# Storing the low parts of the weights from ACT's queue instead of SP's, in a two-layer hybrid trunk

## The chip, the cores and the metric

The kernel runs on one core of a Trainium2 chip. The metric is the device time of one execution in microseconds. The engines are named as in the profile: PE (TensorE, matmul; PEld is its weight load), DVE (VectorE), ACT (ScalarE), POOL (GpSimd) and SP (SyncE, which here only issues DMAs). An engine works through its own list of instructions in order; a DMA is issued from such a list too, so an issue that waits for something holds up what stands behind it on that engine.

## The reference

Two layers over x of 1024 tokens by 1024 channels, all in float32:

```python
h = rms_norm(x, g_pre)
z = h @ w_in            # 3532 columns, split among four mixers
mix = concat(nsa_attention(...)   * silu(gate_a),
             spatial_gating(...)  * silu(gate_b),
             conv_module(...)     * silu(gate_c),    # 31 taps, causal
             rwkv7(...)           * silu(gate_d))    # recurrence over tokens
x = x + rms_norm(mix @ w_out, g_post)
x = x + gated per-layer embedding (two products with weights)
```

The attention has compressed, selected and window branches. RWKV-7 is a recurrence over tokens; in chunks of 64 tokens it needs the inverse of a triangular matrix.

## The kernel before

**Tiling.** Channels lie on partitions. The tokens of each layer l are done in two halves (h=0 and h=1) of 512. Weights come in granules of 128 x 512 elements (256 KB), and every big product is done with three matmuls (`mm3`, L166 to L170): each operand is split into a rounded high part and a low part, and high x high, high x low and low x high are added in PSUM. Such a matmul has the form 128x128 by 128x512.

**A granule** goes through `split_w` (L147 to L164). SP loads it to `ws` (L152), ACT makes the rounded copy `wh` (L158), POOL subtracts to give the low part `wl` (L160). There are three buffers of each. In h=0 the low part is also stored to DRAM (L163, tiles `low0` to `low143`), so that in h=1 SP loads it (L157) instead of POOL making it again. That is 144 stores, 140 of 256 KB and 4 of 152 KB.

**The triangular solve** of RWKV (`rwkv_solve`, L457 to L498) is done once in each half. The matrices go to DRAM (`Nd`) and come back in another layout: four loads of `LB` (L471) and four of `L2` (L476) on SP. DVE does two substitutions: the first over `LB` (L484, L486), the second over `L2` in 16 steps, each a product (L506) and a sum (L508). ACT transposes the results (L492, L510) and issues sixteen small DMAs (`put`, L496) into `Xd`. In `rwkv_tri` SP loads a chunk of the inverse from `Xd` (L536), and the recurrence on PE begins with it (L540, then L547). Its chain has copies on ACT at L527, L595, L602 and L629.

**Other names.** L694 is a tap of the convolution on DVE; L678 and L679 make its input. L976 is ACT's copy of the transposed softmax, which PE multiplies with the values at L981; L1035 is the exponential. L1076 stores intermediate tiles `ped` from ACT's queue.

**Order.** The lists of all engines are set when the kernel is built, by a scheduler which goes by dependencies and priorities; the body of `split_w` has its priority raised by 4000. A DMA also waits for the eighth DMA before it in the list of both queues, since eight semaphores are used in turn.

Of the kernel before, what the change touches and what calls it, by code (L numbers as in the profile page):

```python
# [8 lines left out]
F32 = mybir.dt.float32  # L9
# [32 lines left out]
class Trunk:  # L42
    def __init__(self, ctx, tc, a):
        self.ctx, self.tc, self.nc, self.a = ctx, tc, tc.nc, a
        nc = self.nc
        self.dram = ctx.enter_context(tc.tile_pool(name="dram", bufs=1, space=bass.MemoryType.DRAM))
        self.cp = ctx.enter_context(tc.tile_pool(name="consts", bufs=1))
        self.sb = ctx.enter_context(tc.tile_pool(name="sb", bufs=1))
        self.pp = ctx.enter_context(tc.tile_pool(name="pp", bufs=1, space=bass.MemoryType.PSUM))
        self.n = 0  # L50
        self.nd, self.wide, self.xq, self.xs = 0, None, None, None
        self.low, self.keep = {}, True
        self.setup()

    BUFS = {"aT": 16, "ws": 3, "wh": 3, "wl": 3, "t2": 7, "y": 7, "rv": 2, "pt": 3, "r4": 4, "ab": 8,
# [91 lines left out]
    def split_w(self, src, cols, key, keep):  # L147
        nc = self.nc
        with self.tc.high_priority(offset=4000):
            st = self.t([128, 512], "ws")  # L150
            for ap, w in src:
                nc.sync.dma_start(ap(st), w)  # L152
            hi = self.t([128, 512], "wh", dt=F32R)
            lo = self.t([128, 512], "wl", dt=F32R)
            kept = self.low.get(key)
            if kept is not None:
                nc.sync.dma_start(lo[:, :cols].bitcast(F32), kept)  # L157
            nc.scalar.copy(hi[:, :cols], st[:, :cols])  # L158
            if kept is None:
                nc.gpsimd.tensor_sub(lo[:, :cols], st[:, :cols], hi[:, :cols].bitcast(F32))  # L160
            if kept is None and keep:
                kept = self.low[key] = self.dram.tile([128, cols], F32, name=f"low{len(self.low)}")
                nc.sync.dma_start(kept, lo[:, :cols].bitcast(F32))  # L163
        return hi, lo  # L164

    def mm3(self, out, lh, ll, rh, rl, first, last, shared=False):  # L166
# [1165 lines left out]
```

## Time and profile before

| what | us |
|---|---|
| median of 3 runs | 1803.48 (1800.02 to 1820.78) |
| the profiled execution | 1808.38 |
| its span in the trace | 1806.7 |
| PE busy | 1680.6 (93%) |
| DVE busy | 1210.3 (67%) |
| ACT busy | 796.9 (44%) |
| POOL busy | 398.4 (22%) |
| SP's queue waiting at the stores L163 | 365.5 |

Issues of DMAs don't count as busy. A wait is put down to the instruction whose end came last before the waiting one began. Idle time of an engine that PE does not wait for costs nothing. The mean granted clock of TensorE in this execution was 0.965 of full speed (2.4 GHz); 0.5 is its lower level.

### The profile page before, as it was taken

To read this page: it belongs to the slowest core of one execution; us is meant where nothing else is said; L and a number is where in the kernel's file an instruction comes from. 1 tells how busy PE (TensorE), PEld (TensorE's weight loads), DVE (VectorE), ACT (ScalarE), POOL (GpSimd) and SP (SyncE) were. 2 spreads that over 40 slices of the span, in tenths; PEclk is the share of its full clock that TensorE was granted. 3 is DMA by queue.
4 is the path that set the end of the run, shared out by engine and by line. 5 is a ranking of instruction groups with operands and counts; after the bars stand their busy time and mean duration, and the time that the engine had idled before them with its cause. 6 is when DMAs were issued, how large, how long until landed. Compare 5 with 4: busy or idle time off the path is not lost. (4 is left out here: it accounts for less than half of the span.)

```text
span 1806.7 us, 29182 instructions
## 1 busy us (share of the span) xinstructions
PE 1680.6 (93%) x10068; PEld 1238.0 (69%) x10068; DVE 1210.3 (67%) x3217; ACT 796.9 (44%) x1801; POOL 398.4 (22%) x327
## 2 busy tenths in 40 slices
PE   5998899999999999989988989999999999989988
PEld 3676666667767766767766767766677766667777
DVE  5649898764988645775498871657569885565263
ACT  4432244553233555555322444646342346554453
POOL 3333233000000233422333323000000102323443
PEclk9998899999999999999998989999999899999999
DMA  8467453336753422863664455763486333114554
GB/s 271 135 175 166 135 154 114 91 92 154 201 171 104 142 93 78 264 180 94 169 149 122 144 173 181 231 191 94 115 210 175 108 86 111 48 50 138 180 169 122
DMA packets 361419, 261.19 MB, mean 145 GB/s; under 512 B 84652, under 2 KB 296624, under 8 KB 361272
## 3 DMA queue, kind: packets, MB, share of 16 engines
q1 hardware_dynamic: 318520, 245.17, 46.5%
q10 hardware_dynamic: 42752, 14.16, 3.1%
q8 instruction: 79, 1.29, 0.3%
q14 instruction: 68, 0.56, 0.1%
HBM read 191.50 MB, written 67.77 MB: 144 GB/s over the span
## 5 line engine op out<-in xcount | busy, mean ns | idle before, releaser
L168 PE MATMUL mm<-aT,wh 128*128 128x512 f32 (+1 forms) x1304 | 538.1, 415 | 17.5 <-DVE y L659 4.9
L169 PE MATMUL mm<-aT,wh 128*128 128x512 f32 (+1 forms) x1304 | 531.9, 409 | 3.2 <-DVE aT L258 3.1
L170 PE MATMUL mm<-aT,wl 128*128 128x512 f32 (+1 forms) x1304 | 528.9, 406 | 0.8 <-POOL wl L160 0.3
L158 ACT CAST wh<-ws 128x512 fp32r<-128x512 f32 (+2 forms) x388 | 237.0, 612 | 497.4 <-PE mm L169 301.2
L160 POOL TENSOR_TENSOR wl<-ws,wh 128x512 fp32r<-128x512 f32 (+1 forms) x228 | 305.6, 1343 | 670.7 <-ACT wh L158 560.2
L168 PEld LDWEIGHTS mm<-aT,wh 128*128 128x128 f32 (+1 forms) x1304 | 249.7, 192 | 81.0 <-DVE y L659 5.6
L169 PEld LDWEIGHTS mm<-aT,wh 128*128 128x128 f32 (+1 forms) x1304 | 249.9, 192 | 58.4 <-DVE aT L258 9.1
L170 PEld LDWEIGHTS mm<-aT,wl 128*128 128x128 f32 (+1 forms) x1304 | 249.4, 191 | 53.0 <-issue 2.2
L694 DVE SCALAR_TENSOR_TENSOR cv<-cv,cw,cv 128x512 f32<-128x512 f32 x240 | 196.8, 839 | 1.8
L1035 ACT ACTIVATE r<-s,sma 128x512 f32<-128x512 f32 (+3 forms) x192 | 105.6, 554 | 66.0 <-DVE sma L1033 62.6
L976 ACT COPY pt<-pt 128x512 f32<-128x512 f32 (+1 forms) x152 | 80.4, 529 | 95.2 <-PE pt L973 94.3
L973 PE MATMUL pt<-cst,r 128*128 128x128 f32 x528 | 102.1, 292 | 10.8 <-DVE r L1040 9.4
L981 PE MATMUL pv<-pt,vs 128*64 128x128 f32 x1056 | 93.5, 290 | 1.3 <-ACT pt L976 0.7
L973 PEld LDWEIGHTS pt<-cst,r 128*128 128x128 f32 x528 | 60.3, 142 | 49.0 <-issue 25.5
L981 PEld LDWEIGHTS pv<-pt,vs 128*64 128x64 f32 x1056 | 55.8, 137 | 55.4 <-ACT pt L976 43.2
L1025 DVE CUSTOM_DVE_ANT_0 s<-s,T 128x256 f32<-128x256 f32 (+1 forms) x144 | 54.0, 377 | 42.8 <-PE s L1006 41.9
L1005 PE MATMUL s<-kv,qs 128*128 128x512 f32 (+2 forms) x192 | 75.5, 396 | 2.3 <-ACT r L1035 2.2
L1040 DVE TENSOR_SCALAR r<-r,sma 128x640 f32<-128x640 f32 (+7 forms) x128 | 71.1, 555 | 0.9
L1006 PE MATMUL s<-kv,qs 128*128 128x512 f32 (+2 forms) x192 | 67.0, 353 | 0.0
L608 POOL TENSOR_TENSOR q<-SB,gc 128x256 f32<-128x256 f32 x28 | 22.5, 803 | 196.6 <-DVE SB L621 154.9
L750 POOL TENSOR_SCALAR_AFFINE_SELECT ld<-ld 128x512 f32<-128x512 f32 x4 | 3.0, 752 | 266.9 <-DMA ld<-in_sgu_ln_g_dram 152.5
L249 POOL TENSOR_TENSOR smc<-smc,mhalf 128x1 f32<-128x1 f32 (+1 forms) x28 | 23.2, 830 | 171.4 <-DVE smc L247 107.7
(328 smaller groups left out, 2669.5 us busy)
## 6 DMA issues: line engine op xcount, KB each, us to landing
ws<-in_w_in_dram SPq DMA_DIRECT2D x232, 256.0 KB, 3.3
wl<-low SPq DMA_DIRECT2D x156, 256.0 KB, 3.0
low<-wl SPq DMA_DIRECT2D x140, 256.0 KB, 2.1
ws<-in_ple_gate_dram SPq DMA_DIRECT2D x64, 256.0 KB, 3.0
ws<-in_w_out_dram SPq DMA_DIRECT2D x60, 256.0 KB, 3.0
ped<-ot ACTq DMA_DIRECT2D x32, 256.0 KB, 4.4
ld<-in_nsa_w_dram SPq DMA_DIRECT2D x32, 256.0 KB, 3.4
ld<-ped SPq DMA_DIRECT2D x32, 256.0 KB, 3.3
```

The costliest lines, as they stand in the source:

```text
L158: nc.scalar.copy(hi[:, :cols], st[:, :cols])
L160: nc.gpsimd.tensor_sub(lo[:, :cols], st[:, :cols], hi[:, :cols].bitcast(F32))
L168: nc.tensor.matmul(out, lh, rh, start=first, stop=False, skip_group_check=shared)
L169: nc.tensor.matmul(out, lh, rl, start=False, stop=False, skip_group_check=shared)
L170: nc.tensor.matmul(out, ll, rh, start=False, stop=last, skip_group_check=shared)
L694: nc.vector.scalar_tensor_tensor(ac, xg[j][:, k:k + TH], cw[:, j * 31 + k:j * 31 + k + 1], ac, op0=OP.mult, op1=OP.add)
L973: nc.tensor.transpose(pt[:, o:o + 128], P[e][:, (b + x - b0) * 128:(b + x - b0) * 128 + 128], self.ident)
L976: nc.scalar.copy(PT[:, :n], pt[:, :n])
L981: nc.tensor.matmul(acc[e], w.VS[hh][:, tt, br], PT[:, o:o + 128], start=False, stop=br == 1 and b + x == i, skip_group_check=True)
L1005: nc.tensor.matmul(p[:, :n], w.QS[hd][:, qs], w.KH[br, hh][:, c0 * 128:c1 * 128], start=True, stop=False)
L1035: nc.scalar.activation(P[:, o:o + wd], p[:, c:c + wd], AF.Exp, bias=ng[:, 0:1], accum_out=den[:, x:x + 1])
L1040: nc.vector.tensor_scalar(P[:, :n], P[:, :n], r, None, op0=OP.mult)
```

## The change

The store of a granule's low part is not issued in the call of `split_w` that makes it. The call keeps it in `self.late`, and the next call issues it, behind its own copy and subtraction, on ACT's queue (`nc.scalar`). Five lines are added, so all lines from L164 on are five higher in the new kernel (L496 becomes L501, L540 becomes L545).

```diff
@@ -49,7 +49,7 @@
         self.pp = ctx.enter_context(tc.tile_pool(name="pp", bufs=1, space=bass.MemoryType.PSUM))
         self.n = 0
         self.nd, self.wide, self.xq, self.xs = 0, None, None, None
-        self.low, self.keep = {}, True
+        self.low, self.keep, self.late = {}, True, None
         self.setup()
 
     BUFS = {"aT": 16, "ws": 3, "wh": 3, "wl": 3, "t2": 7, "y": 7, "rv": 2, "pt": 3, "r4": 4, "ab": 8,
@@ -160,7 +160,12 @@
                 nc.gpsimd.tensor_sub(lo[:, :cols], st[:, :cols], hi[:, :cols].bitcast(F32))
             if kept is None and keep:
                 kept = self.low[key] = self.dram.tile([128, cols], F32, name=f"low{len(self.low)}")
-                nc.sync.dma_start(kept, lo[:, :cols].bitcast(F32))
+                late = kept, lo[:, :cols].bitcast(F32)
+            else:
+                late = None
+            if self.late is not None:
+                nc.scalar.dma_start(*self.late)
+            self.late = late
         return hi, lo
 
     def mm3(self, out, lh, ll, rh, rl, first, last, shared=False):
```

The list of SP gets shorter by the 144 stores (and by some waits merged into neighbours), from 1027 rows to 881, ACT's goes from 1586 to 1731 rows. The scheduler does not keep the order of the code.

ACT at the end of the solve of layer 0, h=0 (`q4` is the result of the second substitution, `q5` its transpose, `q1` and `q2` those of the first, `t2` the convolution's input, `kch` the attention's compressed keys). Before:

```order
L158 CAST wh_397_1927<-ws_396_1925 128x512
L678 ACTIVATE t2_372_1795<-mm_373_1796 128x512
L158 CAST wh_400_1947<-ws_399_1945 128x512
L158 CAST wh_405_1972<-ws_404_1970 128x512
L678 ACTIVATE t2_387_1881<-mm_388_1882 128x512
L158 CAST wh_408_1992<-ws_407_1990 128x512
L510 COPY q5_209_971<-q4_207_924 128x128
L158 CAST wh_413_2016<-ws_412_2014 128x512
L496 DMA Xd0_85<-q4_207_924 32x16x8
L496 DMA Xd0_85<-q5_209_971 32x8x16
```

ACT at the same place, in the new kernel:

```order
L158 CAST wh_397_1926<-ws_396_1924 128x512
L501 DMA Xd0_85<-q1_208_928 32x16x16
L167 DMA low30_1930<-wl_398_1927 128x512
L901 ACTIVATE kch_273_1295<-pt_272_1292 64x31
L902 ACTIVATE kch_273_1295<-pt_272_1292 64x31
L683 ACTIVATE t2_372_1794<-mm_373_1795 128x512
L515 COPY q5_209_970<-q4_207_923 128x128
L501 DMA Xd0_85<-q4_207_923 32x16x8
L501 DMA Xd0_85<-q5_209_970 32x8x16
L501 DMA Xd0_85<-q4_207_923 32x16x8
L501 DMA Xd0_85<-q5_209_970 32x8x16
L501 DMA Xd0_85<-q4_207_923 32x16x8
```

The store of a granule (`low30`, from the low part of the granule that was copied to `wh_397`) stands two rows behind that granule's own copy; the solve's copy (now L515) stands ahead of the copies of three granules that stood before it. Two rows further on, behind the copy `wh_400` and one row ahead of the last put, stands the next store, `low31`.

SP where it loads the matrices of the same solve (`q1` is `LB`, `l2` is `L2`). Before:

```order
L163 DMA low21_1202<-wl_257_1199 128x512
L152 DMA ws_374_1797<-in_w_in_dram 128x4x128
L471 DMA q1_203_878<-Nd0_83 32x16x16 x2
L163 DMA low22_1229<-wl_263_1226 128x512
L152 DMA ws_377_1817<-in_w_in_dram 128x4x128
L471 DMA q1_203_878<-Nd0_83 32x16x16
L163 DMA low23_1249<-wl_266_1246 128x512
L152 DMA ws_381_1839<-in_w_in_dram 128x4x128
L471 DMA q1_203_878<-Nd0_83 32x16x16
L476 DMA l2_205_884<-Nd0_83 32x32x16
```

SP at the same place, in the new kernel:

```order
L152 DMA ws_374_1796<-in_w_in_dram 128x4x128
L476 DMA q1_203_877<-Nd0_83 32x16x16 x3
L152 DMA ws_377_1816<-in_w_in_dram 128x4x128
L476 DMA q1_203_877<-Nd0_83 32x16x16
L481 DMA l2_205_883<-Nd0_83 32x32x16
L152 DMA ws_381_1838<-in_w_in_dram 128x4x128
```

The stores are gone, and one weight load instead of two stands between the four loads of `LB`.

DVE at the end of the second substitution of that solve (`cv` is the convolution's sum). Before:

```order
L506 TENSOR_TENSOR q3_206_893<-l2_205_884,q4_207_924 128x232
L694 SCALAR_TENSOR_TENSOR cv_752_3357<-cv_370_1792,cw_3_99,cv_752_3357 128x512
L508 TENSOR_REDUCE q4_207_924<-q3_206_893 128x8
L694 SCALAR_TENSOR_TENSOR cv_752_3357<-cv_370_1792,cw_3_99,cv_752_3357 128x512
L506 TENSOR_TENSOR q3_206_893<-l2_205_884,q4_207_924 128x240
```

DVE at the same place, in the new kernel:

```order
L511 TENSOR_TENSOR q3_206_892<-l2_205_883,q4_207_923 128x232
L513 TENSOR_REDUCE q4_207_923<-q3_206_892 128x8
L511 TENSOR_TENSOR q3_206_892<-l2_205_883,q4_207_923 128x240
L513 TENSOR_REDUCE q4_207_923<-q3_206_892 128x8
L511 TENSOR_TENSOR q3_206_892<-l2_205_883,q4_207_923 128x248
```

The convolution's instructions between the steps have moved behind the substitution.

## Rows read from the trace of the kernel before

**Rows 1.** The page, busy time of each engine.

```profile
PE 1680.6 (93%) x10068; PEld 1238.0 (69%) x10068; DVE 1210.3 (67%) x3217; ACT 796.9 (44%) x1801; POOL 398.4 (22%) x327
```

**Rows 2.** Waits of PE: us in total, times, longest.

```profile
PE rp L540 <- DMA x<-Xd: 10.5, 5, 4.6
...
PE mm L170 <- POOL wl L160: 0.6, 2, 0.3
```

**Rows 3.** Waits of SP's queue: us in total, times, longest.

```profile
SPq L163 <- POOL wl L160: 365.5, 134, 11.8
```

**Rows 4.** Timeline of SP, at a store: start, us, engine, line, operation.

```profile
945.38 0.33 SPq L163 DMA_DIRECT2D low<-wl  x1
945.81 0.38 SPq L152 DMA_DIRECT2D ws<-in_w_in_dram  x1
```

**Rows 5.** The line of the stores: count, ns min/median/max, first and last start.

```profile
L163 SPq DMA_DIRECT2D low<-wl x144: 319/326/542, 23.4 to 1062.7; - x144
```

**Rows 6.** Timeline of SP at the first solve.

```profile
122.06 0.87 SPq L471 DMA_DIRECT2D q<-Nd  x2
...
126.59 0.57 SPq L471 DMA_DIRECT2D q<-Nd  x1
```

**Rows 7.** Timeline of DVE at the end of that solve.

```profile
169.47 0.74 DVE L694 SCALAR_TENSOR_TENSOR cv<-cv,cw,cv 128x512 f32<-128x512 f32 x1
170.13 0.63 DVE L506 TENSOR_TENSOR q<-l,q 128x248 f32<-128x248 f32 x1
```

**Rows 8.** Timeline of PE at layer 1's recurrence; [idle before <-releaser].

```profile
946.44 0.39 PE L168 MATMUL mm<-aT,wh 128*128 128x512 f32 x1
946.67 0.39 PE L169 MATMUL mm<-aT,wh 128*128 128x512 f32 x1
...
952.60 0.69 PE L540 MATMUL rp<-x,at 64*64 64x64 f32 x8 [4.63 <-DMA x<-Xd]
```

**Rows 9.** Timeline of PE at layer 0's recurrence.

```profile
173.15 0.47 PE L168 MATMUL mm<-aT,wh 128*128 128x512 f32 x1 [1.92 <-DVE cv L679]
...
175.15 0.63 PE L169 MATMUL mm<-aT,wh 128*128 128x512 f32 x1
175.57 0.63 PE L170 MATMUL mm<-aT,wl 128*128 128x512 f32 x1
...
183.53 0.45 PE L540 MATMUL rp<-x,at 64*64 64x64 f32 x8 [3.03 <-DMA x<-Xd]
...
189.22 0.69 PE L547 MATMUL rp<-x,q 64*64 64x64 f32 x8 [2.72 <-DVE q L543]
```

**Rows 10.** A line whose stores are on ACT's queue already.

```profile
L1076 ACTq DMA_DIRECT2D ped<-ot x32: 326/327/754, 17.7 to 1757.5; - x32
```

**Rows 11.** Stretches with stores: us, ACT busy, granted clock, DMA share, GB/s.

```profile
20.00:292.00 272.00, 98.01 (x205) 0.95 0.59 166
604.00:688.00 84.00, 50.18 (x132) 1.00 0.40 126
721.00:1063.00 342.00, 135.82 (x295) 0.96 0.55 159
```

**Rows 12.** Timeline of ACT, two granules.

```profile
150.68 0.62 ACT L158 CAST wh<-ws 128x512 fp32r<-128x512 f32 x1 [2.08 <-DMA Xd<-q]
...
153.40 0.62 ACT L158 CAST wh<-ws 128x512 fp32r<-128x512 f32 x1 [2.10 <-PE mm L169]
```

**Rows 13.** Timeline of POOL beside it.

```profile
151.38 1.29 POOL L160 TENSOR_TENSOR wl<-ws,wh 128x512 fp32r<-128x512 f32 x1 [1.41 <-ACT wh L158]
```

**Rows 14.** Waits of all engines: us in total, times, longest.

```profile
ACT wh L158 <- PE mm L169: 301.2, 160, 12.0
...
PEld pv L981 <- ACT pt L976: 43.2, 116, 0.8
```

**Rows 15.** PE in two stretches behind those waits, same columns.

```profile
184.00:195.00 11.00, 8.28 (x30) 0.53 0.28 83
952.00:970.00 18.00, 15.88 (x74) 0.53 0.32 101
```

## The prediction

> **What bounds the kernel now.** I read the page first [rows 1]: TensorE (PE) is busy for 1680.6 us of the span of 1806.7, so at most 126 us can be won by ending its waits; ACT is busy 44% and POOL 22%. Next, the waits of PE [rows 2]: of what the stores' granules give it, PE waits for POOL's low part 0.6 us in all. The largest repeated wait that this change can reach is the one of the RWKV recurrence (L540) for the load of its inverse, 10.5 us in five waits. Then the SP queue [rows 3]: it stands 365.5 us in front of stores (L163) that want POOL's subtraction, 134 times. It looks as if that wait should be worth a lot. Whether it is, is read from the timeline of SP [rows 4]: behind the store at 945.38 the next weight load starts at 945.81, and so it goes on at each granule. That load reuses a buffer that the same subtraction was the last to read (three buffers, and the list runs three granules ahead), so with the store gone it waits for the same event, at most one issue (0.33 us) less. The wait changes its name, and PE did not wait for the weights anyway.
>
> **SP's side.** 144 stores with a median of 0.326 us of issue [rows 5] leave SP: 144 x 0.326 = 47 us, all of it beside PE's work. What covers it are the loads three granules ahead. Gain 0; the bound on the gain is the 0.6 us of [rows 2].
>
> **The loads of the solve.** Between the matrices of the triangular solve SP had stores and the loads behind them [rows 6]: the four L471 loads start from 122.06 (two of them) to 126.59. In the new order three of the four stand together, and only one weight load comes between. The last can start at about 123.4 (122.06 + 0.87 + one issue of 0.4), 3.2 us earlier.
>
> **DVE's and PE's order at the two first-half solves.** With that the scheduler also lists the solve's second chain (L506/L508, which the diff moves to L511/L513) without convolution taps in between: 13 (layer 0) and 15 (layer 1) instructions fewer between its 32. Each tap L694 adds 0.66 us there (169.47 to 170.13) [rows 7], so the chain ends about 13 x 0.66 + 3.2 = 12 us earlier in layer 0 and 10 to 13 us in layer 1. But PE's list moves L540 up as well: from matmul 478 to 427 (51 earlier) and from 2340 to 2299 (41 earlier). Matmuls start 0.227 us apart [rows 8], so PE asks 51 x 0.227 = 11.6 and 41 x 0.227 = 9.3 us earlier. Supply and demand move by the same amount, and the waits of 3.03 and 4.63 us [rows 8, 9] stay of that kind. Bounds: both gone, -7.7 us; the chain not earlier at all, +20.9. I take -4: half of the waits, since the estimates for the chain are 0.4 to 4 us better than PE's move.
>
> **ACT's side: issue.** 144 x 0.327 us, which is what an equal store takes on ACT's queue now (L1076, [rows 10]): 47 us. ACT works 98.01 + 50.18 + 135.82 = 284 us of the 698 us in which the stores fall (56 in the first of these stretches, 16 in the second, 72 in the third) [rows 11], 41%, so the room is there.
>
> **ACT's side: waiting.** This is the term to look at. The order of the new kernel does not have each store behind the next granule's copy: in 140 of 144 it stands behind its own granule's copy and ahead of the next, with no instruction between in 36 cases, one in 67, two in 38 and three in 3. The subtraction starts 0.08 us behind the copy's end and takes 1.29 us [rows 12, 13], so a store directly behind its copy holds ACT's queue for 1.37 us. With one instruction of some 0.6 us between I count 0.75, with two 0.2: 36 x 1.37 + 67 x 0.75 + 38 x 0.2 = 107 us. With the 47 of issue it is 154 us, in ACT's idle 414.
>
> Who stands behind the store? In 52 cases the next copy L158. Copies wait 301.2 us, 160 times, for PE to give a buffer free [rows 14], 1.9 us each, and at PE's pace a granule comes every 2.72 us (150.68 and 153.40 in [rows 12]); copy, subtraction and issue take 0.62 + 1.37 + 0.33 = 2.32 of that. Hidden, by 0.4 us, and if that cover goes (a late store before it) PE still has two more granules in hand. In some 48 cases it is an instruction of the convolution, a put of the solve or the like, for which nobody waits at once. In some 44 it is one that PE needs soon: the softmax and its transposed copy (L1035, L976), the chain of the recurrence (L527, L595, L602, L629). Their mean hold is 107/144 = 0.74 us and with the issue 1.07: 47 us. PE's weight load for L981 waits 116 times for L976 now, but 0.37 us in the mean and at most 0.8 [rows 14]; the matmul itself hides it. **Bounds** of this term: 0 (ACT would have waited for its own operands anyway) and 44 x 1.37 = 60 us (each full hold ends in PE). I take one part in six of the 47, +8, nearest to the row of L981: PE runs so near behind ACT only in places, and ACT is busy only 41% of the time.
>
> The store also waits for the eighth transfer before it, in most cases a weight load long landed. In a few (low35, low37, low45, low47) this is a load of the solve or a prefetch that SP may hold; I count nothing and leave it to a rival.
>
> **Sum.** 0 - 4 + 8 = +4 us. The profiled execution took 1808.38 us (span 1806.7), 4.9 above the median of 1803.48; +4 on 1808.38 is 1812, on the scale of the median 1807.5. I give **1808**.
>
> The Trainium skill, in "DMA: Bandwidth & Descriptors", section "Issuing engines are not separate DMA queues", says that issuing from another engine saves only the sequencer's time for the issue, since all transfers interleave on the same sixteen DMA engines. By that rule alone the sum could reach down to -47, if every issue on SP had lain on the path; by the row on PE's waits for the low part it is -0.6 at most, and the row decides here.
>
> **Rivals.**
>
> *The recurrence's places get clean (faster).* For it: the solve's loads and chain come 10 to 13 us earlier, and the waits around the two places are 1.92, 3.03, 2.72 us [rows 9] and 4.63 us [rows 8], 12.3 in all, and behind them PE has a granted clock of 0.53 (the lower level, 1.2 GHz) for about 11 + 18 = 29 us [rows 15], in which matmuls start 0.43 us apart (175.15 to 175.57, [rows 9]) in place of 0.227: 29 x (1 - 0.227/0.43) = 14 us. All gone, and ACT's term 0: 1803.5 - 12.3 - 14 = 1777. Against it: PE's list moves by the same time as the chain, and one short wait there is enough for the slow stretch. Chance 0.10.
> The Trainium skill's "Perfetto Trace Analysis", section "DMA Optimizations", speaks for this side: it advises giving inputs and outputs issuing engines of their own. By the rows only the solve's loads could profit.
>
> *PE asks too early.* PE's order moves L540 up by 11.6 and 9.3 us, but the chain gains less, because on ACT the copies and puts of the solve (L510, L496) now stand behind stores that wait for POOL: low30 ahead of the copy, low31 ahead of the last put, 1.37 us each. If the chain gains 5 us less than PE asks at each of two places, that is 10 us of waits, and some 8 us more at the low clock cost 4: 1803.5 + 4 + 14 = about 1821. Chance 0.20.
>
> *ACT's queue becomes the bound (slower).* The mechanism: the store's wait, in front of L976, L1035 and the recurrence's chain, where PE's order has nothing else ready, plus the stores that wait for the eighth transfer before them while SP holds it. It decides from the point at which 36 of the 60 to 107 us of holds end in PE. At 47 us: 1803.5 + 47 = about 1851. For it: PE needs L976 within 0.8 us of its end [rows 14]. Against it: ACT idles 59%, and copies that wait for PE absorb the rest. Chance 0.09.
>
> *The change does what its words say.* If the stores did stand behind the next copy, their subtraction would be long done, no hold would be left, ACT's term would be 0 and the solve's -4 to -6: about 1798. The printed order speaks against it; 0.03.
>
> **How the numbers follow.** Forecast 1808 with 0.58, its own range 1793 to 1817. With the second rival (1821, up to 1832) and the last (1798) it holds 0.81; the first and third are left out below and above: 1783 to 1832. A change of under 2%, 36 us, is about what a measurement of this kernel can't tell from none: 1767 to 1839. Faster than that: 1767 lies 10 us under the first rival, so half of its chance, 0.05; slower: the third rival's 0.09; same 0.86.
>
> **What the next profile would show.** Right: no L163 on SP, and SP's wait for POOL not gone but standing at L152; ACT's share up by nothing, since issues don't count as busy, but its queue holding stores that wait for the subtraction, over 60 us in all; PE's busy time unchanged within 10 us; at the two places L540 waiting some 2 to 5 us, about 10 us earlier in the program. Wrong, and how: waits of PE or PEld for ACT L976, L1035, L602 grown from some 50 to over 100 us (third rival); L540's waits over 15 us (second); L540 without wait and the clock at 1.00 around both places (first). What would break the whole argument is a change of order somewhere that I have not weighed: the lists of ACT, DVE and PE differ in many rows beside these.

## The result, and the profile after

The changed kernel takes 1861.97 us (median of 4 runs, 1860.76 to 1865.24). Against the kernel before, measured beside it (median 1809.84), the ratio is 1.0303, 95% interval 1.0269 to 1.0337: slower by some 55 us. The forecast was 1808, no change. The profiled execution took 1861.24 us. In the trace lines, ACTq and SPq are the parts of ACT and SP that issue DMAs, and DMA_DIRECT2D is such an issue.

The page of the changed kernel, span and busy time by engine:

```profile
span 1859.5 us, 29162 instructions
...
PE 1695.4 (91%) x10068; PEld 1245.1 (67%) x10068; DVE 1213.3 (65%) x3217; ACT 800.0 (43%) x1801; POOL 399.2 (21%) x327
```

Every engine does the work that it did before [rows 1]. PE has 15 us more of busy time, though it runs the same matmuls: its mean granted clock is 0.957 instead of 0.965. The rest of the 53 us of span, 38 us, is idle time of PE. ACT's busy share says nothing of what happened, because a queue that stands at a DMA issue counts as idle.

Waits of PE in the changed kernel (us in total, times, longest; lines are five higher than before):

```profile
PE pt L885 <- ACT t L882: 8.6, 2, 4.5
PE mm L173 <- ACT t L683: 8.6, 2, 4.4
...
PE rp L545 <- DMA x<-Xd: 4.9, 4, 1.7
...
PE mm L173 <- ACT aT L262: 3.8, 4, 2.1
```

PE's waits for ACT, summed over all lines of this view, rise from 31.8 us (23 times) to 63.2 (45 times); for DVE from 67.1 to 73.2. The new ones are small and scattered: the input of the convolution (L683), copies for transposes (L882), copies of activations (L262). New means here only that the kernel before has less of them; which of them the stores cause is separated further down. The weights themselves are still in time. The wait of the recurrence for its inverse fell from 10.5 us [rows 2] to 4.9.

Waits of SP's queue in the changed kernel, same columns:

```profile
SPq L152 <- POOL wl L160: 695.9, 223, 14.4
```

The line of the stores in the changed kernel (count, ns min/median/max, first and last start):

```profile
L167 ACTq DMA_DIRECT2D low<-wl x144: 326/398/405, 23.4 to 1122.2; - x144
```

Waits of all engines in the changed kernel, the row of PE's weight load behind ACT's softmax copy:

```profile
PEld pv L986 <- ACT pt L981: 44.7, 115, 1.3
```

SP's wait for POOL did not go; it moved from the stores [rows 3] to the loads behind them, 224.0 us in 80 waits before and 695.9 in 223 now. An issue on ACT has a median of 0.398 us, not 0.327 [rows 10]. The wait that I had watched, L981 for L976, has hardly moved: 44.7 us after 43.2 [rows 14].

How a store holds ACT is seen where ACT's timeline is laid beside POOL's. ACT in the changed kernel, at the first solve (start, us, [idle before <-releaser]):

```profile
169.24 0.62 ACT L158 CAST wh<-ws 128x512 fp32r<-128x512 f32 x1 [2.44 <-PE mm L175]
...
171.61 0.41 ACTq L167 DMA_DIRECT2D low<-wl  x1
172.11 0.62 ACT L158 CAST wh<-ws 128x512 fp32r<-128x512 f32 x1 [2.25 <-DMA Xd<-q]
...
174.19 0.41 ACTq L167 DMA_DIRECT2D low<-wl  x1
174.64 0.49 ACTq L501 DMA_DIRECT2D Xd<-q  x1
175.23 0.62 ACT L158 CAST wh<-ws 128x512 fp32r<-128x512 f32 x1 [2.50 <-DMA Xd<-q]
...
177.27 0.41 ACTq L167 DMA_DIRECT2D low<-wl  x1
177.73 0.19 ACT L901 ACTIVATE kch<-pt 64x31 fp32r<-64x31 f32 x1 [1.88 <-POOL wl L160]
...
178.14 0.60 ACT L683 ACTIVATE t<-mm 128x512 f32<-128x512 f32 x1
```

POOL in the same stretch of the changed kernel:

```profile
169.99 1.59 POOL L160 TENSOR_TENSOR wl<-ws,wh 128x512 fp32r<-128x512 f32 x1 [1.76 <-ACT wh L158]
172.86 1.30 POOL L160 TENSOR_TENSOR wl<-ws,wh 128x512 fp32r<-128x512 f32 x1 [1.29 <-ACT wh L158]
175.98 1.26 POOL L160 TENSOR_TENSOR wl<-ws,wh 128x512 fp32r<-128x512 f32 x1 [1.82 <-ACT wh L158]
```

PE there, changed kernel:

```profile
178.79 0.50 PE L173 MATMUL mm<-aT,wh 128*128 128x512 f32 x1 [4.19 <-ACT t L683]
```

ACT and POOL run in lockstep: copy, subtraction, store, next copy. Each store starts 0.03 us after its subtraction ends (171.58, 174.16, 177.24), and nothing behind it on ACT can start earlier. Copies come 2.87 and 3.12 us apart, where before they came 2.72 apart, at PE's pace [rows 12]. The convolution's input L683, which needs nothing from POOL, stands behind three such stores and comes at 178.14; PE has waited 4.19 us for it. In an ACT view most of this reads as idle time with a copy's or a DMA's name on it; only the store's row and the end of POOL's row beside it show the hold. The place shows what a hold looks like; how much it costs there is another question, which the experiments answer. Summed over the 144 stores, the time from the end of ACT's instruction ahead of a store to the end of its issue is 208 us. This sum is called the holds from here on.

The loads of the first solve on SP in the changed kernel:

```profile
141.12 1.68 SPq L476 DMA_DIRECT2D q<-Nd  x3
...
143.48 0.51 SPq L476 DMA_DIRECT2D q<-Nd  x1
```

PE where the two recurrences begin, changed kernel:

```profile
193.29 0.45 PE L545 MATMUL rp<-x,at 64*64 64x64 f32 x8 [1.61 <-DMA x<-Xd]
...
999.49 0.45 PE L545 MATMUL rp<-x,at 64*64 64x64 f32 x8 [1.74 <-DMA x<-Xd]
```

From the first to the last load of `LB` it takes 2.36 us instead of 4.53 [rows 6], which is 2.2 us less where 3.2 were forecast, and the waits at L540 (L545 in the new kernel) fell from 3.03 and 4.63 us [rows 8, 9] to 1.61 and 1.74. That part came much as forecast, but 10 and 47 us later in the program (193.29 against 183.53, 999.49 against 952.60), not 10 earlier: so much had been lost by then.

### The profile page after: what moved, and what is told of

The parts are those of the page before. It is cut to its first block, busy times and chain, and to the rows that moved or that the text cites. A ratio compares the mean times of both kernels' runs of the same rounds, so it can differ in the third digit from the quotient of the medians.

```text
span 1859.5 us, 29162 instructions
## 1 busy us (share of the span) xinstructions
PE 1695.4 (91%) x10068; PEld 1245.1 (67%) x10068; DVE 1213.3 (65%) x3217; ACT 800.0 (43%) x1801; POOL 399.2 (21%) x327
## 5 line engine op out<-in xcount | busy, mean ns | idle before, releaser
L699 DVE SCALAR_TENSOR_TENSOR cv<-cv,cw,cv 128x512 f32<-128x512 f32 x240 | 191.5, 815 | 2.9
L981 ACT COPY pt<-pt 128x512 f32<-128x512 f32 (+1 forms) x152 | 80.6, 530 | 102.3 <-PE pt L978 94.0
L986 PEld LDWEIGHTS pv<-pt,vs 128*64 128x64 f32 x1056 | 55.8, 137 | 56.4 <-ACT pt L981 44.7
L1042 DVE TENSOR_TENSOR sma<-sma 128x1 f32<-128x1 f32 x64 | 17.6, 274 | 67.5 <-ACT r L1040 67.3
```

Source lines behind the costliest of these rows:

```text
L699: nc.vector.scalar_tensor_tensor(ac, xg[j][:, k:k + TH], cw[:, j * 31 + k:j * 31 + k + 1], ac, op0=OP.mult, op1=OP.add)
L981: nc.scalar.copy(PT[:, :n], pt[:, :n])
L986: nc.tensor.matmul(acc[e], w.VS[hh][:, tt, br], PT[:, o:o + 128], start=False, stop=br == 1 and b + x == i, skip_group_check=True)
```

## The experiments

The lists of instructions come first. Without the deferral, with the store issued from ACT where the code before issues it from SP, the program's lists are the changed kernel's row for row; with the deferral but on SP they are those of before. So the deferral has no effect on the program, and the change consists of one word, and it has two effects: the stores hold ACT, and the lists of PE, DVE and ACT come out in another order. To separate the two, the lists are pinned in what follows. Every kernel below has this addition, with a table of the wanted order (shortened: the unpacking of the table and the prefixes of names are left out):

```diff
     Trunk(ctx, tc, a).run()
+    ins = list(tc.nc.cur_bb.bb.instructions)
+    for mine in LISTS:                     # one per engine
+        for p, q in zip(mine, mine[1:]):   # issue order alone, no wait
+            tc.add_manual_dep(ins[q], ins[p].name, DependencyInfo(
+                DependencyClass.NoSync, DependencyReason.DATA), reason="list")
```

and, where the stores are ACT's, `nc.scalar.dma_start` for `nc.sync.dma_start` at L163 (no deferral). Only the table differs between them otherwise. Ratios are to the kernel before, measured beside each.

### Lists or holds

**Changed lists, stores back on SP.**

> The lists of PE, DVE, ACT, POOL and SP are pinned to those of the changed kernel, only the 144 stores are taken off ACT's list and put back on SP, each ahead of the weight load it stood ahead of before. Theory 1 (ACT's queue is held by stores that wait for POOL): the loss is gone, 1803 to 1818 us. Theory 2 (the new lists of PE, DVE and ACT are worse in themselves, whoever issues the stores): it stays, 1845 to 1865 us. Half and half would give some 1830.

Measured: 1824.16 us, ratio 1.0082 (1.0061 to 1.0104). The new lists cost some 15 us by themselves, so theory 2 holds for a part; more than two thirds of the loss went with the stores.

**Lists of before, stores on ACT at the changed kernel's distances.**

> The lists of PE, DVE, ACT, POOL and SP are pinned to those of the kernel before; only the stores go from SP to ACT, each as many instructions behind its own granule's copy as in the changed kernel (0 to 3). Theory 1 (holds on ACT): slow like the changed kernel, 1845 to 1870 us. Theory 2 (lists): like before, 1800 to 1815 us.

Measured: 1894.28 us, ratio 1.0476 (1.0448 to 1.0504), above the range of theory 1. With the lists of before, holding ACT costs some 86 us. With the scheduler's new order, 15 us dear by itself, the whole loss is some 30 us less than that. Waits of PE in this kernel:

```profile
PE rp L540 <- DMA x<-Xd: 17.5, 4, 9.3
...
PE s L1005 <- ACT r L1035: 8.0, 9, 1.9
```

The recurrence's wait for its inverse grows from 10.5 us [rows 2] to 17.5; the solve's copies and puts stand behind stores on ACT in this list.

**Changed lists, each store behind the next granule's copy.** On ACT's list, for each store:

```diff
 L158 copy of granule n
-L163 store of granule n      (0 to 3 instructions behind its copy)
 ...
 L158 copy of the next granule
+L163 store of granule n
```

> The changed kernel's lists, pinned, but each store moved on ACT's list to the place right behind the next granule's copy, as the change's words have it. Theory 1 (holds): a store's subtraction is done by then, so most of the loss goes, 1805 to 1825 us. Theory 2 (lists): 1845 to 1865 us. Theory 3 (the 144 issues of some 0.4 us themselves fill ACT): 1845 to 1865 us too.

Measured: 1823.13 us, ratio 1.0095 (1.0075 to 1.0115). One place further back on ACT's list, and the stores cost no more than on SP (1.0082). This refutes theory 3: the same 144 issues stand on ACT, where they now take 0.327 us in the median. Of holds, 17 us are left of the 208. The page of this kernel:

```profile
span 1820.8 us, 29160 instructions
...
PE 1679.8 (92%) x10068; PEld 1238.0 (68%) x10068; DVE 1200.9 (66%) x3217; ACT 799.3 (44%) x1801; POOL 394.6 (22%) x327
```

Beside the changed kernel: 1859.5 - 1820.8 = 38.7 us of span, of which 15.6 are PE's busy time (1695.4 - 1679.8, the same matmuls at a mean granted clock of 0.957 instead of 0.963) and 23.1 its idle time.

**Lists of before, each store behind the next copy.**

> The lists of before, pinned, with the stores on ACT right behind the next granule's copy. Theory 1: no holds, 1800 to 1815 us, possibly a little under the kernel before, since SP is free of 144 issues. Theory 2: 1800 to 1815 us. Theory 3 (issue time on ACT): 1830 to 1860 us.

Measured: 1807.89 us, ratio 1.0022 (1.0004 to 1.004). As theory 1 has it, though no gain: SP without 144 issues and their waits is worth nothing.

**The changed kernel, pinned to its own lists.**

> The changed kernel with its own lists pinned: 1858 to 1866 us, as without pins, in any theory. Another time would mean that the pins cost or give something, and the kernels with pins could not be read against the changed one.

Measured: 1857.83 us, ratio 1.0287 (1.0252 to 1.0322), within the interval of the unpinned one. The pins can be left out of account.

### What the stores were worth in the kernel before

**136 of 144 stores left out** (the edit is shortened). The first four of each size are stored, and all later loads of low parts read these, so the products of the second half are not the reference's.

```diff
+                had = [v for v in self.low.values() if v.shape[-1] == cols]
+                if len(had) < 4:
                     kept = self.low[key] = self.dram.tile(...)
                     nc.sync.dma_start(kept, lo[:, :cols].bitcast(F32))
+                else:
+                    self.low[key] = had[len(self.low) % 4]
```

> The lists of before, pinned, with 136 of the 144 stores left out altogether; the second half's loads read the same number of bytes from the eight low parts that are stored (so the output is not the reference's). By the prediction SP's issues and waits at the stores are worth nothing: 1798 to 1806 us. Rival (SP's 365 us of waits, or the traffic of 36 MB, cost time in the kernel before): under 1790 us.

Measured: 1804.93 us, ratio 0.9992 (0.9961 to 1.0023). Taking the stores away wins nothing clear of the noise: by the lower end of the interval 0.4%, some 7 us, is the most that another place for them could win. SP's 365 us of waits, 47 us of issue and the stores' traffic lay beside the work.

**Stores on POOL, behind their own subtraction** (`nc.gpsimd.dma_start`, lists of before).

> The lists of before, pinned, with each store on POOL's list directly behind its own subtraction, so that it holds neither SP nor ACT. If any queue that is idle does, it takes the time of before, 1800 to 1812 us. If POOL's issue is dear (the trace shows no store of its own there), the next subtraction comes late and with it the weights: over 1820 us. Under 1795 us if SP's order had cost anything, which the kernel without stores speaks against.

Measured: 1815.43 us, ratio 1.0065 (1.0045 to 1.0086), between the two expectations. An issue there keeps POOL itself busy for a median of 0.562 us; the line of the stores in this kernel:

```profile
L163 POOL DMA_DIRECT2D low<-wl x144: 557/562/812, 23.2 to 1074.8; - x144
```

### Which holds

All of these have the changed kernel's lists; a store either keeps its place (held) or stands behind the next copy. The three classes are those of the prediction.

> The changed kernel's lists, pinned. Of its stores only the 52 that stand directly ahead of a next rounding copy keep their place on ACT's list; the other 92 stand behind the next copy. The reference for all three kernels of this kind is 1823 us (all behind the next copy), the changed kernel is 1862. By the prediction these holds are hidden by the copies' own wait for PE: 1821 to 1826 us. Rival (every hold counts alike, 52 of 144): 1823 + 14 = 1837 us.

> As above, but only the 44 stores keep their place that stand ahead of an instruction which I called one that PE soon needs (softmax, transposed copies, chain of the recurrence). By the prediction +8: 1831 us (bounds 0 and 47). Rival (every hold alike): 1823 + 12 = 1835 us.

> As above, but only the other 48 stores keep their place (ahead of inputs of the convolution and of the projections, puts of the solve, key and value copies). By the prediction nobody waits for these at once: 1821 to 1826 us. Rival (every hold alike): 1823 + 13 = 1836 us. Third view: most of the 38 us lie here, since these read the PSUM banks that PE's next products need and feed what PE's list has right behind: over 1843 us.

> Changed kernel's lists, pinned; the 52 stores ahead of a copy and the 48 ahead of the others keep their place on ACT's list, the 44 ahead of instructions that PE soon needs stand behind the next copy. Alone the two classes cost some 2 and 8 us over the 1823 of none. If the losses add: 1833 us. If the cover of the copies is used up by the holds in between (slack shared, so that losses grow faster than holds): 1842 us or more.

> The same with the 44 and the 48 in place and the 52 ahead of a copy moved. Alone they cost some 3 and 8 us. If the losses add: 1834 us. If the slack is shared: 1842 us or more.

> The same with every second store in place in the order of ACT's list, of whatever class (72), the other 72 behind the next copy. If each hold costs its part: half of 38, 1842 us. If the loss comes from holds that follow each other granule after granule: a good deal less than half, 1826 to 1834 us.

> The changed kernel's lists, pinned; the first 72 stores of ACT's list (all of layer 0) keep their place, the last 72 stand behind the next copy. If it counts that holds follow each other: about half of the 38 us, 1838 to 1848 us, where the same number alternating gave some 6 us (1827 to 1829). If it counts only how many there are: 1826 to 1832 us as for the alternating ones.

> The same with the last 72 (layer 1) in place and the first 72 moved. If holds that follow each other count: 1835 to 1848 us, and the losses of both halves add up to some 38. If the number counts: 1826 to 1832 us.

> Eight stores in place, eight moved, in turn over ACT's list (72 in place). If following each other counts: nearer to the halves, 1834 to 1846 us. If the number counts: 1826 to 1832 us.

| held | stores | us | ratio to before (interval) | above none, in % |
|---|---|---|---|---|
| none | 0 | 1823.13 | 1.0095 (1.0075 to 1.0115) | 0 |
| ahead of a copy | 52 | 1827.81 | 1.0105 (1.0078 to 1.0132) | 0.10 |
| ahead of what PE soon needs | 44 | 1830.07 | 1.0111 (1.0056 to 1.0165) | 0.16 |
| ahead of others | 48 | 1837.68 | 1.0140 (1.0098 to 1.0182) | 0.45 |
| copies and others | 100 | 1846.13 | 1.0242 (1.0211 to 1.0273) | 1.47 |
| soon and others | 92 | 1851.46 | 1.0262 (1.0230 to 1.0294) | 1.67 |
| every second | 72 | 1827.11 | 1.0128 (1.0102 to 1.0154) | 0.33 |
| eight and eight | 72 | 1843.89 | 1.0209 (1.0171 to 1.0247) | 1.14 |
| the first 72 | 72 | 1845.00 | 1.0209 (1.0172 to 1.0247) | 1.14 |
| the last 72 | 72 | 1841.24 | 1.0182 (1.0143 to 1.0221) | 0.87 |
| all (changed kernel) | 144 | 1861.97 | 1.0303 (1.0269 to 1.0337) | 2.08 |

By the ratios none of the first three differs from "none" by more than the intervals of both together, so none of them alone is shown to be a loss, and the third view of the others (over 1843) is refuted. By the rule "every hold counts alike" the three should have cost 14, 12 and 13 us. In pairs the classes cost more than their sum: 1.47 against 0.55, 1.67 against 0.61. How much more is uncertain. With the plain medians of all runs of a series in place of the ratios (the kernel before has 1806.54 in the series of the single classes, 1804.19 in that of "none", 1803.21 in that of the pairs), the three classes come to 0.13, 0.25 and 0.67, and the pairs to 1.33 and 1.63: 1.7 times the sum. The class of the others is the one that moves. The holds themselves do add up: the kernels with one class held have 86, 75 and 74 us of them, which less the 17 of none is 69, 58 and 57, and with the 17 again 201 of the changed kernel's 208.

The four kernels with 72 held stores are clearer. Alternating, 72 holds cost 0.33%; in runs of eight, or as one half of the program, they cost 0.87 to 1.14%, and the two halves together (2.01) make up the whole (2.08). It is not that the alternating stores hold for much less: their holds sum to 101 us, those of the runs of eight to 110 and of the halves to 112 each. So it matters whether holds follow each other. Only one of the two alternations was run; that the 72 other stores would cost as little is not shown.

**Where the holds cost.** The changed kernel and that with each store behind the next copy have the same lists, so their matmuls can be compared one by one. Of the 38.6 us by which the last matmul is later, 16.8 arise over the first 400 matmuls, from 13 to 128 us, and 15.8 between the 4200th and the 5000th, from 766 to 940 us. Some 53 of the 144 stores lie in these two stretches, with 75 of the 208 us of holds. The other 91 stores hold ACT for 133 us, and all that is outside the two stretches costs 6. The same two stretches in four traces (us from to, us, busy time of PE with matmuls, granted clock, DMA share, GB/s): each store behind the next copy,

```profile
13.01:111.30 98.29, 86.28 (x400) 0.95 0.58 172
742.13:900.77 158.64, 148.50 (x801) 0.99 0.51 157
```

the changed kernel,

```profile
13.15:128.25 115.10, 95.89 (x400) 0.87 0.50 148
766.02:940.46 174.44, 158.53 (x802) 0.93 0.47 142
```

the alternating kernel,

```profile
13.26:115.59 102.33, 89.01 (x400) 0.92 0.55 165
748.22:908.78 160.56, 150.53 (x801) 0.98 0.51 156
```

and runs of eight, in an execution that was the slowest of its four and 6 us over their median:

```profile
13.76:120.69 106.93, 92.66 (x400) 0.89 0.52 158
756.55:931.57 175.02, 160.23 (x802) 0.91 0.46 142
```

In the second stretch the alternating kernel has 25 us of holds and the kernel with runs of eight 27; against "none" the first loses 1.9 us there and the second 16.4. So in the same place the same amount of holds costs little one by one and much in a row. But following each other is not enough. In the changed kernel all stores are held, and the 36 that come after the second stretch, with 54 us of holds, cost nothing: behind the 5000th matmul no more time is lost. These are comparisons of one execution each; the pinned kernel gives 15.3 and 16.4 us for the two stretches, too.

What a hold does in the second stretch of the changed kernel is seen at the input of the recurrence. ACT:

```profile
899.59 0.69 ACT L401 ACTIVATE t<-c,der 128x512 f32<-128x512 f32 x1 [0.62 <-PE c L399]
901.02 0.40 ACTq L167 DMA_DIRECT2D low<-wl  x1
901.52 0.63 ACT L407 ACTIVATE t<-t 128x512 f32<-128x512 f32 x1 [1.24 <-DVE t L402]
```

DVE behind it, and PE, and the granted clock after that (columns as above):

```profile
902.19 0.17 DVE L410 COPY gc<-t 128x8 f32<-128x8 f32 x1 [0.92 <-ACT t L407]
...
912.30 1.10 PE L433 MATMUL rp<-y,cst 128*128 128x512 f32 x2 [2.94 <-DVE y L430]
...
915.00:920.00 5.00, 5.00 (x15) 0.50 0.00 0
```

With the store behind the next copy, ACT goes straight on to the same instruction, DVE does not wait, and PE waits 0.49 us at that place:

```profile
867.20 0.62 ACT L402 ACTIVATE t<-t 128x512 f32<-128x512 f32 x1
...
876.87 1.10 PE L428 MATMUL rp<-y,cst 128*128 128x512 f32 x2 [0.49 <-DVE y L425]
...
876.00:896.00 20.00, 18.82 (x123) 1.00 0.42 111
```

So a store that holds ACT for a good microsecond reaches PE by way of DVE, and behind PE's wait of 2.94 us its matmuls run at the lower level of the clock for a while. DVE's wait of 0.92 us and one of 0.35 right behind it make up half of the 2.45 us that PE waits longer here; where the other half comes from was not followed. Over the two stretches PE's busy time grows by 19.6 us (234.8 to 254.4, the same matmuls) and its idle time by 13.0.

## Why the prediction was wrong

**What bounds the kernel, SP's side: right.** SP's wait went to the next load, and the stores are worth nothing there (0.9992 without them).

**The solve's loads, DVE's and PE's order: right in the place, wrong as a price of the lists.** The waits at L540 fell by 1.42 and 2.89 us, 4.3 together, where I had taken -4; they also fell in the kernel with the same lists and no holds, to 4.9 us in all. But I took the lists' effect to be these two places, and the lists differ everywhere. With the stores on SP they cost 0.82%, some +15 us. I had named this as what would break the argument, and gave it no term and no chance. In the trace of the kernel with stores behind the next copy, PE's waits for ACT are 52.7 us (33 times) against 31.8 before; the wait that grew most is the one for the copy L877, which does not show before at all:

```profile
PE pt L880 <- ACT t L877: 10.5, 2, 5.3
...
PE rp L428 <- DVE y L425: 1.6, 3, 0.7
```

Which of the moved rows makes up the 15 us was not tried and stays open.

**ACT's side, issue: right.** 144 issues on ACT cost nothing that can be measured when nothing is held by them (1.0095 against 1.0082 on SP, 1.0022 with the lists of before).

**ACT's side, waiting: this is the step that failed.** I took +8 of bounds 0 and 60; measured is 2.08 points, some 38 us (35 by the pinned kernel) of the 55; the lists make up the rest. That is within the bounds, but the value rested on three readings of which none stood:

1. The holds were too short. I counted 107 us of waits and 47 of issue, 154; measured are 208. In the trace a store right behind its copy holds for 1.93 us in the mean, with one instruction between for 1.44 and with two for 1.03, where I had 1.70, 1.08 and 0.53 with the issue. So an instruction between its own copy and the store covers less than I gave it.
2. The turnaround was too short. I had 0.62 + 1.37 + 0.33 = 2.32 us per granule against PE's 2.72 and called it hidden. In the trace it is 2.87 and 3.12 at the first solve: the subtraction took up to 1.59, the issue 0.41, and a put of 0.49 stood between. That this costs time there is not shown: the changed kernel is 17 us behind the kernel without holds at its 400th matmul (128 us) and 15 at its 800th (215 us), and this place lies between them.
3. I priced each store by who stands directly behind it, asked only whether PE waits for that one, and added. Single classes cost 2, 3 and 8 us by the ratios, none of them clear of the noise; that makes 13 us of 38, or 19 by the plain medians. What is missing in the sum comes from holds in a row, in two stretches of the program. At the place that was followed there, what ACT makes late goes by DVE to PE, and a longer slow stretch of PE comes with it; my sum had no such way and no such price.

The waits by name bear this out. Against the kernel with the same lists and no holds, the changed kernel has 10.5 us more of PE's waits for ACT (63.2 after 52.7) and 9.5 more for DVE (73.2 after 63.7). The largest rise is PE's wait for DVE's `y`:

```profile
PE rp L433 <- DVE y L430: 9.3, 3, 3.3
```

It was 1.6 us without holds. The wait at L683 rises from 3.8 to 8.6. The copy L882, which looks like the stores' work in a comparison with the kernel before, was at 10.5 us without any hold and belongs to the new lists, as does most of what ACT's waits gained. So the forecast watched the wrong place (L981, 44.7 us after 43.2) and the wrong engine: nearly half of the added waits carry DVE's name.

That holds in a row are dearer than holds apart is shown by the four kernels with 72, and most directly by the second stretch. Why they are is only argued: ACT's lead over PE absorbs one hold and not several. No kernel with a shorter subtraction was run.

**The rivals.** "ACT's queue becomes the bound" had chance 0.09 and 1851 us; it names the right queue and mechanism (ACT held by stores), but the wrong place (in front of the softmax and inside the recurrence's chain); of the 208 us of holds some 38 ended in the time, close to its 36. That its 1851 us lies nearest to what was measured is partly luck, since it has no term for the new lists. "PE asks too early" did not come with the changed lists, but did with those of before (17.5 us at L540). "The change does what its words say" was tried by moving the stores: 1823 with the changed lists, 1808 with those of before. A store behind the next copy would have been free with the lists of before, but the scheduler did not keep the deferral. The rule of the Trainium skill's page "DMA: Bandwidth & Descriptors", section "Issuing engines are not separate DMA queues", that another issuing engine saves only the issue's time, agrees with 1.0022, the kernel in which nothing but the issues moved; here that time was not on the path, and what the other engine loses the rule does not say.

## What to carry to other kernels

A DMA that waits for another engine's result belongs on a queue that has nothing else to do. On a compute engine it turns two engines that overlapped into a lockstep, and the price is not the sum of the holds by who stands behind them: here 53 of 144 stores made five sixths of the cost. Ask where a late result travels on to the bound engine, by a third engine too, and whether holds follow each other there. Before costing a deferral, look in the printed order whether it survived the scheduler; and where lists change everywhere, give the new order a term of its own, with both signs. To see what a hold costs, compare with a kernel of the same lists and not with the kernel before: the comparison with before puts waits of the new order down to the stores.

## What the runs showed of the hardware that was not expected

The same store's issue took a median of 0.398 us on ACT when it was released by a subtraction that had just ended, 0.327 us on ACT when its data had long been there, and 0.562 us on POOL, where it counts as busy. From issue to landing the stores took a median of 3.3 us from ACT (page of the changed kernel) and 2.1 from SP before. About two fifths of the cost of the holds (15.6 of 38.7 us) is not waiting but the same matmuls at a lower mean clock; in the two stretches that carry the loss it is 19.6 of 32.6 us. A wait of 2.94 us at 912.30 was followed by the lower level from 915 to 920 us, where the kernel without the wait stayed at 1.00.
